# Small unused tiles between the moving tiles of the feed-forward products

## The chip, the core and the metric

The program runs on one core of one Trainium2 chip. The metric is the device time of one execution in microseconds; lower is better. TensorE (PE in the profile) multiplies; VectorE (DVE), ScalarE (ACT) and GpSimd (POOL) work element by element; SyncE (SP) issues most DMAs. Operands lie in SBUF, 128 partitions of some 200 KB each; "an address" below is a tile's byte offset within its partition, the same on all 128.

## The reference, cut to what matters

Two layers, each with a feed-forward, a mixing of tokens (three kinds of attention or recurrence, not touched here), and a second feed-forward. There are 512 tokens, a width of 1024 and an inner width of 2816:

```
def _swiglu(h, wg, wu, wd):
    return (jax.nn.silu(h @ wg) * (h @ wu)) @ wd
...
h = _rmsnorm(x, ffn1_norm[i])
x = x + 0.5 * _swiglu(h, ffn1_w_gate[i], ffn1_w_up[i], ffn1_w_down[i])
h = _rmsnorm(x, mix_norm[i])
x = x + _mixing(h, positions, w_in[i], w_out[i], ...)
h = _rmsnorm(x, ffn2_norm[i])
x = x + 0.5 * _swiglu(h, ffn2_w_gate[i], ffn2_w_up[i], ffn2_w_down[i])
```

All is float32. The four feed-forwards are most of the arithmetic.

## The kernel before

Everything stays transposed: features on the partitions, the 512 tokens along the free axis. To keep float32 precision with a faster product, every operand is split in two float32r tiles, a high part (`xh`, `hh`, `wh`) and the rest (`xl`, `hl`, `wl`), and a product is made of three matmuls (`mm3`, lines 250 to 252): high times high, rest of the data times high weights, and high data times rest of the weights. In each the weights are the stationary operand, a slice of 128 x 128 that one LDWEIGHTS loads, and the data is the moving operand, 128 x 512, that streams past them: 2,048 bytes of each partition, while a slice of weights is 512 bytes.

A feed-forward (`ffn`) has two stages. In the first, for each of 22 blocks of the inner width, the gate and the up product are accumulated (`gu_ps`): 8 slices of the width, three matmuls each, so 24 matmuls for an output and 1,056 for a feed-forward. The moving tiles are the 16 tiles `xh0`, `xl0`, ..., `xh7`, `xl7`. VectorE and ScalarE make the pair `hh`, `hl` of each block out of them. In the second stage, for each of 8 blocks of the width, the down product is accumulated (`d_ps`) over the 22 blocks: 66 matmuls for an output, 528 for a feed-forward; its moving tiles are the 44 tiles `hh0`, `hl0`, ..., `hh21`, `hl21`. `load_split` brings a block of weights (`raw`, three buffers), and ScalarE and VectorE split it (lines 243 and 245) into `wh` and `wl`, two buffers each, of 4,096 bytes; a priority puts these splits ahead of other work, and a scheduler orders the rest.

In the mixing stage the same `xh` and `xl` are the moving operand of `proj_d` (`hf_ps`, `hq_ps`, `fq_ps`, `fk_ps`), 512 columns; in `proj_t` (`hg_ps`, `hi_ps`, `dqk_ps`, `dv_ps`, `fv_ps`) the roles are exchanged: slices of `xh` and `xl` are the stationary operand and a row of `wh` or `wl` of 256 columns moves (260 for `fv_ps`, where a row is 1,040 bytes). The output product (`o_ps`) moves tiles of the mixing stage itself.

The pools lay their tiles one behind another in the order of the code, so addresses follow from sizes. `PAD`, an unused tile at the head of the first pool, shifts all of them together. In the built program they are:

```
        xh0     xl0     xh1    ...  xl7     wh (two)       wl (two)        hh0      hl0      hh1
before  43008   45056   47104  ...  73728   88064, 92160   96256, 100352   124288   126336   128384
after   41696   43776   45856  ...  72896   87232, 91328   95424,  99520   123488   125568   127648
```

Before, the tiles `xh` and `xl` stand whole multiples of 2,048 bytes from the weights, and the tiles `hh` and `hl` multiples of 2,048 plus 1,408. Slices of the weights start every 512 bytes, so what can differ between matmuls is the distance modulo 512: it is 0 for every `xh` and `xl`, and 384 for every `hh` and `hl`. The tiles that `o_ps` moves stand at 128 or 384.

Of the kernel before, what the change touches and what calls it, by code (L numbers as in the profile page):

```python
# [10 lines left out]
F32 = mybir.dt.float32  # L11
# [14 lines left out]
LEVELS = (1, 2, 4, 8, 16, 32, 64)  # L26
AHEAD = 400
CHAIN = 100
PAD = 352


def shape_constants():
# [95 lines left out]
def hybrid_trunk(ctx: ExitStack, tc: tile.TileContext, a, out):  # L128
# [4 lines left out]
    keep = ctx.enter_context(tc.tile_pool(name="keep", bufs=1))  # L133
# [13 lines left out]
    def acc(name):  # L147
        return acc_p.tile([128, 512], F32, tag="acc", name=name)
# [4 lines left out]

    const.tile([128, PAD], F32, name="pad")
    x = [keep.tile([128, T], F32, name=f"x{k}") for k in range(KB)]
# [12 lines left out]
    pos = lines(const, [128, NB], I32, name="pos")  # L168
    xh = [None] * KB
    xl = [None] * KB  # L170

    ones = const.tile([128, 128], F32, name="ones")
    V.memset(ones, 1.0)

    def norm_block(k, g, nrm):

        split_block(k, g)
        square_block(k, nrm)

    def split_block(k, g):  # L180
        xh[k] = keep.tile([128, T], R32, tag=f"xh{k}", name=f"xh{k}")
        S.activation(xh[k], x[k], AF.Copy, scale=g)
        xl[k] = keep.tile([128, T], R32, tag=f"xl{k}", name=f"xl{k}")
        V.scalar_tensor_tensor(out=xl[k], in0=x[k], scalar=g, in1=xh[k].bitcast(F32),  # L184
                               op0=ALU.mult, op1=ALU.subtract)
# [48 lines left out]
    def load_split(src, n, cols):  # L234

        if raws:
            raw = raws.pop(0)
        else:
            raw = wp.tile([128, n, cols], F32, tag="raw", name="raw", bufs=3)
            nc.sync.dma_start(out=raw, in_=src)  # L240
        with tc.high_priority(AHEAD):
            wh = wp.tile([128, n, cols], R32, tag="wh", name="wh")
            S.copy(wh, raw)  # L243
            wl = wp.tile([128, n, cols], R32, tag="wl", name="wl")
            V.tensor_tensor(out=wl, in0=raw, in1=wh.bitcast(F32), op=ALU.subtract)  # L245
        return wh, wl

    def mm3(ps, lh, ll, rh, rl, first, last):

        PE.matmul(ps, lh, rh, start=first, stop=False)  # L250
        PE.matmul(ps, lh, rl, start=False, stop=False)  # L251
        PE.matmul(ps, ll, rh, start=False, stop=last)  # L252
# [8 lines left out]
    for k in range(KB):  # L261
        split_block(k, gvec(("ffn1_norm", 0), k))
# [103 lines left out]
    def ffn(l, wg, wu, wd, after, rb, early=None):  # L366
        with tc.tile_pool(name="ffn", bufs=1, reuse_waits="tile") as fp:
            hh, hl = [], []
            for j in range(FB):
                if j == 4 and early:  # L370
                    early()
                part = []
                for w in (wg, wu):
                    wh, wl = load_split(w[l, j], KB, 128)
                    ps = acc("gu_ps")
                    for k in range(KB):
                        mm3(ps, wh[:, k, :], wl[:, k, :], xh[k], xl[k], k == 0, k == KB - 1)
                    part.append(ps)
                g = fp.tile([128, T], F32, tag="g", name="g", bufs=2)
                V.tensor_tensor(out=g, in0=part[0], in1=rb, op=ALU.mult)  # L380
                S.activation(g, g, AF.Silu)
                u = fp.tile([128, T], F32, tag="u", name="u", bufs=2)
                V.tensor_tensor(out=u, in0=part[1], in1=rb, op=ALU.mult)  # L383
                V.tensor_tensor(out=u, in0=u, in1=g, op=ALU.mult)  # L384
                h1 = fp.tile([128, T], R32, name=f"hh{j}")
                S.copy(h1, u)  # L386
                h2 = fp.tile([128, T], R32, name=f"hl{j}")
                V.tensor_tensor(out=h2, in0=u, in1=h1.bitcast(F32), op=ALU.subtract)  # L388
                hh.append(h1)
                hl.append(h2)  # L390
            for d in range(KB):
                ps = acc("d_ps")
                for j0, j1 in ((0, 8), (8, 15), (15, 22)):
                    wh, wl = load_split(wd[l, d, :, j0:j1, :], j1 - j0, 128)
                    for j in range(j0, j1):
                        mm3(ps, wh[:, j - j0, :], wl[:, j - j0, :], hh[j], hl[j], j == 0, j == FB - 1)
                V.scalar_tensor_tensor(out=x[d], in0=ps, scalar=0.5, in1=x[d], op0=ALU.mult, op1=ALU.add)  # L397
                after(d)
# [361 lines left out]
    for l in range(L):  # L760
        nrm = {}
        ffn(l, a["ffn1_w_gate"], a["ffn1_w_up"], a["ffn1_w_down"],
            lambda d: norm_block(d, gvec(("mix_norm", l), d), nrm), rb, None if l else tables)
        r, rb = norm_finish(nrm)
        nrm = {}
        with ExitStack() as ctx2:
            mixing(l, lambda d: norm_block(d, gvec(("ffn2_norm", l), d), nrm), r, rb)
        r, rb = norm_finish(nrm)
        nrm = {}
        if l + 1 < L:  # L770
            ffn(l, a["ffn2_w_gate"], a["ffn2_w_up"], a["ffn2_w_down"],
                lambda d: norm_block(d, gvec(("ffn1_norm", l + 1), d), nrm), rb)
            r, rb = norm_finish(nrm)
        else:
            def last(d):
                square_block(d, nrm)
                if d == KB - 2:
                    warm = lines(small, [128, 1], tag="warm", name="warm")
                    S.activation(warm, nrm["ss"][:, 0:1], AF.Sqrt)

            ffn(l, a["ffn2_w_gate"], a["ffn2_w_up"], a["ffn2_w_down"], last, rb)
            _, rb = norm_finish(nrm, copy=False)
            for d in range(KB):
                V.scalar_tensor_tensor(out=x[d], in0=x[d], scalar=gvec("final", d), in1=rb,
                                       op0=ALU.mult, op1=ALU.mult)
                (nc.scalar if d % 2 else nc.sync).dma_start(out=out[d * 128:(d + 1) * 128, :], in_=x[d])
# [17 lines left out]
```

## Time and the profile before

| | us |
|---|---|
| median of the two runs | 2114.78 (2114.63 to 2114.94) |
| the profiled execution | 2115.02 |
| its span, first to last instruction | 2113.2 |
| PE busy | 2085.1 (99%) |
| DVE busy | 993.3 (47%) |
| ACT busy | 691.9 (33%) |

The span is the stretch in which the profile sees instructions; the execution has 1.8 us around it. A matmul's duration in the profile is longer than the time it takes from its neighbours, because the next one starts before it has ended: what a matmul costs in a dense stretch is the time from its start to the next one's start, which can be had from the first and the last start of a group and their number.

### The profile page before, as it was taken

To read this page: it belongs to the slowest core of one execution; us is meant where nothing else is said; L and a number is where in the kernel's file an instruction comes from. 1 tells how busy PE (TensorE), PEld (TensorE's weight loads), DVE (VectorE), ACT (ScalarE), POOL (GpSimd) and SP (SyncE) were. 2 spreads that over 40 slices of the span, in tenths; PEclk is the share of its full clock that TensorE was granted. 3 is DMA by queue.
4 is the path that set the end of the run, shared out by engine and by line. 5 is a ranking of instruction groups with operands and counts; after the bars stand their busy time and mean duration, and the time that the engine had idled before them with its cause. 6 is when DMAs were issued, how large, how long until landed. Compare 5 with 4: busy or idle time off the path is not lost.

```text
span 2113.2 us, 25262 instructions
## 1 busy us (share of the span) xinstructions
PE 2085.1 (99%) x10358; PEld 1728.6 (82%) x10358; DVE 993.3 (47%) x1640; ACT 691.9 (33%) x1039; POOL 12.7 (1%) x18
## 2 busy tenths in 40 slices
PE   8999999999999999999999999999999999999997
PEld 6888888889877888888888888889888778888885
DVE  7544433556454544443344443335655454444323
ACT  5323222333443433222233322222344443223221
POOL 0000000000000000000000000000000000000000
PEclk9999999999999999999999999999999999999998
DMA  5333333211122333333333333332111223333332
GB/s 171 100 91 99 95 93 97 90 60 41 31 88 63 94 96 100 100 94 91 95 98 92 100 99 93 93 100 72 60 46 46 65 80 95 100 91 98 93 95 72
DMA packets 55092, 183.71 MB, mean 87 GB/s; under 512 B 7216, under 2 KB 7344, under 8 KB 54976
## 3 DMA queue, kind: packets, MB, share of 16 engines
q1 hardware_dynamic: 54368, 180.98, 28.4%
q8 instruction: 81, 1.33, 0.3%
q10 hardware_dynamic: 576, 1.05, 0.1%
q14 instruction: 35, 0.29, 0.0%
q0 software_dynamic: 32, 0.07, 0.0%
HBM read 179.94 MB, written 2.10 MB: 86 GB/s over the span
## 4 chain that ended last, share of the span: by engine, by line
PE 97%; DVE 1%; ACT 1%; issue 1%; DMA 0%; DVEq 0%; SPq 0%; ACTq 0%
PE gu_ps L251 15%; PE gu_ps L252 15%; PE gu_ps L250 15%; PE d_ps L250 8%; PE d_ps L252 8%; PE d_ps L251 8%; PE lv_ps L510 2%; PE sc_ps L561 2%; PE po L580 2%; PE o_ps L250 1%; PE o_ps L251 1%; PE o_ps L252 1%; PE ho_ps L696 1%; PE pt_ps L573 1%; PE hg_ps L434 1%; PE hg_ps L435 1%
## 5 line engine op out<-in xcount | busy, mean ns | idle before, releaser
L243 ACT CAST wh<-raw 128x1024 fp32r<-128x1024 f32 (+3 forms) x352 | 356.3, 1012 | 1071.7 <-issue 408.4
L245 DVE TENSOR_TENSOR wl<-raw,wh 128x1024 fp32r<-128x1024 f32 (+3 forms) x352 | 413.5, 1175 | 314.0 <-ACT wh L243 311.8
L250 PE MATMUL gu_ps<-xh,wh 128*128 128x512 f32 x1408 | 548.5, 390 | 7.9 <-ACT wh L243 7.9
L252 PE MATMUL gu_ps<-xh,wl 128*128 128x512 f32 x1408 | 550.3, 391 | 0.3 <-DVE wl L245 0.3
L251 PE MATMUL gu_ps<-xl,wh 128*128 128x512 f32 x1408 | 548.0, 390 | 0.0
L250 PEld LDWEIGHTS gu_ps<-xh,wh 128*128 128x128 f32 x1408 | 264.6, 188 | 64.0 <-ACT wh L243 7.9
L252 PEld LDWEIGHTS gu_ps<-xh,wl 128*128 128x128 f32 x1408 | 264.5, 188 | 56.8 <-DVE wl L245 1.5
L251 PEld LDWEIGHTS gu_ps<-xl,wh 128*128 128x128 f32 x1408 | 264.6, 188 | 55.4 <-DVE xl L184 0.2
L252 PE MATMUL d_ps<-hh,wl 128*128 128x512 f32 x704 | 278.1, 395 | 0.0
L250 PE MATMUL d_ps<-hh,wh 128*128 128x512 f32 x704 | 278.1, 395 | 0.0
L251 PE MATMUL d_ps<-hl,wh 128*128 128x512 f32 x704 | 278.1, 395 | 0.0
L383 DVE TENSOR_TENSOR u<-gu_ps,rb 128x512 f32<-128x512 f32 x88 | 60.8, 691 | 269.4 <-PE gu_ps L252 269.4
L252 PEld LDWEIGHTS d_ps<-hh,wl 128*128 128x128 f32 x704 | 132.1, 188 | 32.1
L250 PEld LDWEIGHTS d_ps<-hh,wh 128*128 128x128 f32 x704 | 132.2, 188 | 32.1
L251 PEld LDWEIGHTS d_ps<-hl,wh 128*128 128x128 f32 x704 | 132.2, 188 | 32.0
L380 DVE TENSOR_TENSOR g<-gu_ps,rb 128x512 f32<-128x512 f32 x88 | 60.8, 691 | 177.0 <-PE gu_ps L252 175.1
L386 ACT CAST hh<-u 128x512 fp32r<-128x512 f32 x88 | 54.9, 624 | 64.1 <-DVE u L384 64.1
L397 DVE SCALAR_TENSOR_TENSOR x<-d_ps,x 128x512 f32<-128x512 f32 x32 | 22.1, 691 | 95.4 <-PE d_ps L252 95.4
L384 DVE TENSOR_TENSOR u<-u,g 128x512 f32<-128x512 f32 x88 | 60.9, 692 | 8.3
L388 DVE TENSOR_TENSOR hl<-u,hh 128x512 fp32r<-128x512 f32 x88 | 60.3, 685 | 4.1 <-ACT hh L386 4.1
L510 PE MATMUL lv_ps<-hQ,hk 128*128 128x64 f32 x448 | 54.2, 274 | 2.8 <-DVE hk L521 2.8
L510 PEld LDWEIGHTS lv_ps<-hQ,hk 128*128 128x128 f32 x448 | 52.4, 192 | 5.2 <-PE hi_ps L435 1.3
(242 smaller groups left out, 2360.3 us busy)
## 6 DMA issues: line engine op xcount, KB each, us to landing
raw<-in_ffn_w_gate SPq DMA_DIRECT2D x88, 512.0 KB, 3.5
raw<-in_ffn_w_up SPq DMA_DIRECT2D x88, 512.0 KB, 3.5
raw<-in_ffn_w_down SPq DMA_DIRECT2D x64, 448.0 KB, 3.3
raw<-in_w_in SPq DMA_DIRECT2D x52, 512.0 KB, 3.5
raw<-in_ffn_w_down SPq DMA_DIRECT2D x32, 512.0 KB, 3.5
raw<-in_w_out_dh SPq DMA_DIRECT2D x16, 384.0 KB, 3.0
raw<-in_w_in SPq DMA_DIRECT2D x8, 260.0 KB, 2.7
x<-in_x SPq DMA_DIRECT2D x8, 256.0 KB, 5.7
```

Of the source, the lines that this page charges most:

```text
L243: S.copy(wh, raw)
L245: V.tensor_tensor(out=wl, in0=raw, in1=wh.bitcast(F32), op=ALU.subtract)
L250: PE.matmul(ps, lh, rh, start=first, stop=False)
L251: PE.matmul(ps, lh, rl, start=False, stop=False)
L252: PE.matmul(ps, ll, rh, start=False, stop=last)
L380: V.tensor_tensor(out=g, in0=part[0], in1=rb, op=ALU.mult)
L383: V.tensor_tensor(out=u, in0=part[1], in1=rb, op=ALU.mult)
L384: V.tensor_tensor(out=u, in0=u, in1=g, op=ALU.mult)
L386: S.copy(h1, u)
L388: V.tensor_tensor(out=h2, in0=u, in1=h1.bitcast(F32), op=ALU.subtract)
L510: PE.matmul(ps[:, e:e + 64], K[:, hh, s], Q[:, hh, s].rearrange("p (n two c) -> p n two c", two=2, c=c)[:, :, 1, :], start=True, stop=True)
L561: PE.matmul(ps[:, 0:n], qt(h)[:, b * 128:(b + 1) * 128], kt(h)[:, 0:n], start=True, stop=True)
```

## The change

Tiles of 32 bytes that nothing reads or writes are allocated ahead of every `xh`, `xl`, `hh` and `hl`, and `PAD` goes from 1,408 bytes to 64, which gives room for them. Every such moving tile is now 2,080 bytes behind the one before it. Modulo 512, the distance from the weights is 32 for `xh0`, 64 for `xl0`, 96 for `xh1`, and so on to 0 for `xl7`: each multiple of 32 once. For `hh0` it is 416, for `hl0` 448, and so on through the 44 tiles, each multiple of 32 two or three times. Modulo 64, all tiles stood at 0 before; now `xh` and `hh` stand at 32, and `xl` and `hl` at 0. The tiles of `o_ps` keep their distances from the weights.

```
-PAD = 352
+PAD = 16
...
+    shifted = set()
...
     def split_block(k, g):
+        if k not in shifted:
+            keep.tile([128, 8], F32, name=f"ph{k}")
         xh[k] = keep.tile([128, T], R32, tag=f"xh{k}", name=f"xh{k}")
         S.activation(xh[k], x[k], AF.Copy, scale=g)
+        if k not in shifted:
+            keep.tile([128, 8], F32, name=f"pl{k}")
+            shifted.add(k)
         xl[k] = keep.tile([128, T], R32, tag=f"xl{k}", name=f"xl{k}")
...
+                fp.tile([128, 8], F32, name=f"ph{j}")
                 h1 = fp.tile([128, T], R32, name=f"hh{j}")
                 S.copy(h1, u)
+                fp.tile([128, 8], F32, name=f"pl{j}")
                 h2 = fp.tile([128, T], R32, name=f"hl{j}")
```

No instruction is added to TensorE, ScalarE or SyncE, and on every engine the instructions stand in the same order as before. What is new besides the addresses is one more semaphore that `hl4` waits for on VectorE in the second feed-forward of either layer: its place now overlaps with one that GpSimd has cleared in the mixing stage.

## Rows read from the trace of the kernel before

**Rows 1.** The page: busy time by engine, and the chain that ended last.

```profile
PE 2085.1 (99%) x10358; PEld 1728.6 (82%) x10358; DVE 993.3 (47%) x1640; ACT 691.9 (33%) x1039; POOL 12.7 (1%) x18
...
PE 97%; DVE 1%; ACT 1%; issue 1%; DMA 0%; DVEq 0%; SPq 0%; ACTq 0%
PE gu_ps L251 15%; PE gu_ps L252 15%; PE gu_ps L250 15%; PE d_ps L250 8%; PE d_ps L252 8%; PE d_ps L251 8%; PE lv_ps L510 2%; PE sc_ps L561 2%; PE po L580 2%; PE o_ps L250 1%; PE o_ps L251 1%; PE o_ps L252 1%; PE ho_ps L696 1%; PE pt_ps L573 1%; PE hg_ps L434 1%; PE hg_ps L435 1%
```

**Rows 2.** Busy time of each engine in two stretches of the first feed-forward.

```profile
core 0: us, PE busy (x) PEld busy (x) DVE busy (x) ACT busy (x) POOL busy (x), PEclk, DMA share, GB/s
40.00:240.00 200.00, 200.00 (x884) 165.58 (x884) 99.83 (x160) 63.52 (x81) 0.00 (x0) 1.00 0.32 96
267.00:375.00 108.00, 108.00 (x465) 86.88 (x464) 36.97 (x41) 29.28 (x35) 0.95 (x1) 1.00 0.33 96
```

**Rows 3.** Matmuls into gu_ps, 40 to 240 us: ns min/median/max, first and last start.

```profile
L250 PE MATMUL gu_ps<-xh,wh x295: 389/389/389, 39.8 to 239.7; 128*128 128x512 f32 x148
L251 PE MATMUL gu_ps<-xl,wh x295: 389/389/389, 40.1 to 240.0; 128*128 128x512 f32 x148
L252 PE MATMUL gu_ps<-xh,wl x294: 389/389/389, 40.3 to 239.5; 128*128 128x512 f32 x147
```

**Rows 4.** Matmuls into d_ps, 267 to 375 us.

```profile
L250 PE MATMUL d_ps<-hh,wh x155: 392/392/398, 266.7 to 374.5; 128*128 128x512 f32 x155
L251 PE MATMUL d_ps<-hl,wh x155: 392/398/398, 266.9 to 374.7; 128*128 128x512 f32 x155
L252 PE MATMUL d_ps<-hh,wl x155: 392/392/398, 267.1 to 374.9; 128*128 128x512 f32 x155
```

**Rows 5.** Timeline of PE after a pause, 22.4 to 25.6 us: start, duration.

```profile
22.26 0.36 PE L213 MATMUL ss_ps<-ones,ss 128*128 128x1 f32 x2
22.48 0.48 PE L250 MATMUL gu_ps<-xh,wh 128*128 128x512 f32 x1
22.80 0.40 PE L251 MATMUL gu_ps<-xl,wh 128*128 128x512 f32 x1
23.03 0.40 PE L252 MATMUL gu_ps<-xh,wl 128*128 128x512 f32 x1
...
24.65 0.39 PE L250 MATMUL gu_ps<-xh,wh 128*128 128x512 f32 x1
...
25.55 0.39 PE L251 MATMUL gu_ps<-xl,wh 128*128 128x512 f32 x1
```

**Rows 6.** Matmuls into o_ps, first layer, 615 to 700 us.

```profile
L251 PE MATMUL o_ps<-olA,wh x32: 390/396/481, 622.6 to 683.1; 128*128 128x512 f32 x32
...
L252 PE MATMUL o_ps<-ohd,wl x16: 392/394/690, 621.1 to 680.5; 128*128 128x512 f32 x16
```

**Rows 7.** Matmuls into hf_ps, hi_ps and fv_ps, whole span, by tile.

```profile
L250 PE MATMUL hf_ps<-xh,wh x64: 387/389/578, 375.2 to 1492.1; 128*128 128x512 f32 x64
...
L432 PE MATMUL hi_ps<-wh,xh x128: 277/283/365, 398.9 to 1472.6; 128*128 128x256 f32 x128
...
L432 PE MATMUL fv_ps<-wh,xh x64: 277/282/372, 579.6 to 1636.2; 128*128 128x260 f32 x64
```

**Rows 8.** Matmuls into gu_ps and d_ps, whole span, by tile.

```profile
L250 PE MATMUL gu_ps<-xh,wh x1408: 387/389/796, 7.9 to 1972.8; 128*128 128x512 f32 x176
...
L251 PE MATMUL d_ps<-hl,wh x704: 387/395/399, 252.2 to 2096.2; 128*128 128x512 f32 x176
```

**Rows 9.** Who waited for whom: us in total, times, longest.

```profile
ACT wh L243 <- PE d_ps L251: 274.0, 72, 4.1
DVE u L383 <- PE gu_ps L252: 269.4, 82, 3.4
ACT wh L243 <- PE gu_ps L251: 261.0, 90, 3.4
```

**Rows 10.** Timelines of POOL, 300 to 700 us, and of DVE, 736 to 746 us.

```profile
476.07 0.94 POOL L648 MEMSET fqa<- 2x1024 f32 x1 [11.99 <-DVE hQ L496]
...
737.29 0.69 DVE L388 TENSOR_TENSOR hl<-u,hh 128x512 fp32r<-128x512 f32 x1
```

## The prediction, made before the changed kernel was run

> **What bounds the kernel.** The page comes first: TensorE is busy 99% of the span, and 97% of the chain that ended last is its matmuls, gu_ps and d_ps alone some 68% [rows 1]. The next view asks whether the clock, a DMA or another engine holds it: in both stages of a feed-forward the granted clock is 1.00, so the 2.4 GHz level, PE has no gap, the DMAs are busy about a third of the time, DVE a half and less [rows 2]. The view of waits says the same from the other side: ScalarE, which makes the weights, waits for TensorE to give up a buffer, 261.0 and 274.0 us, and VectorE waits for its results [rows 9]. So each nanosecond on a matmul of a feed-forward is paid in full, and there are 4 x 1,056 = 4,224 into gu_ps and 4 x 528 = 2,112 into d_ps.
>
> What is one worth? The starts tell. In gu_ps, 295 matmuls of line 250 start between 39.8 and 239.7 us, and two others stand between each pair: 199.9 / (294 x 3) = 226.6 ns from start to start; every duration is 389 [rows 3]. In d_ps it is 107.8 / (154 x 3) = 233.3 ns, and the durations are 392 or 398, about half of each [rows 4]. Duration less 162 is the distance to the next start in both (389 gives 227, the mean 395 gives 233), so I read durations in that way below.
>
> The two stages issue the same pair, a load of 128 columns and a matmul of 512, from the same weight buffers, back to back at the same clock. What differs is the place of the moving tile: at distance 0 from the weights (modulo 512) it takes 226.6, at 384 it takes 233.3. That is the best evidence in this trace that the distance has a price, 6.7 ns, which is 16 cycles at 2.4 GHz. The tiles of o_ps, at 128 or 384, show durations of 394 to 396 in the median, thus some 233 ns as well [rows 6].
>
> Distance 0 alone doesn't give the low figure. After a pause, the matmuls into gu_ps that start at 22.80 to 24.65 us take 1.85 / 8 = 231.3 ns each, and only then fall into the even step: 0.90 / 4 = 225, which is 226.6 within the rounding [rows 5]. So there is a settled state at 226.6, reached after some nine matmuls that all stand at the same distance, and a restless one at about 231. All of gu_ps stays settled, as the median of 389 for the whole span shows, with 387 as its smallest [rows 8].
>
> **The change, part by part.** The order of the instructions is the same and TensorE gets none, so nothing is paid for issuing. The new semaphore on hl4 costs nothing: GpSimd's last clearing in the mixing stage starts at 476.07 us and an hl of the second feed-forward is written at 737.29 [rows 10]. Were it late, VectorE's next tensors would queue behind it and then TensorE for its weights, but 260 us cover it. The smaller PAD shifts everything alike; it changes no distance between tiles. Writing the moved tiles is ScalarE's and VectorE's work, which has slack [rows 9].
>
> What remains is the distance. Now two matmuls in a row never have the same one. For gu_ps the trace shows only distance 0; the new ones, each multiple of 32 once, are bounded by the nearest rows: 225 ns (387, the smallest duration seen in either stage) and 236 ns (398, the longer of the two steps of d_ps) [rows 4, 8]. Between them lie 231.3 for matmuls that haven't settled [rows 5] and 233.3 for a settled state at another distance [rows 4]. I expect that a distance which changes with each matmul prevents the settled state at 226.6, and take 232, between these two, as nearest to both. It is a choice; nothing here shows 32, 64 or 96.
>
> - gu_ps: (232 - 226.6) x 4,224 = +22.8 us.
> - d_ps: it loses its 384 for all distances, 0 among them: (232 - 233.3) x 2,112 = -2.7 us.
> - The projections with xh and xl moving, 576 matmuls of 512 columns, have a median of 389 in hf_ps, so about half or more are settled today [rows 7]: 5.4 x 576 x 0.6 = +1.9 us.
> - proj_t, 1,536 matmuls of 256 or 260 columns: the loads are now at other distances. Durations are 283 for hi_ps and, with every second moving row 16 bytes off, 282 for fv_ps, which has 4 columns more [rows 7]. So no price shows there, and I put 0.
> - o_ps keeps its distances: 0.
>
> The sum is +22.0 us on the profiled execution's 2115.02, which is 0.24 over the median of the runs: **2137 us**, 1.0% slower. With the bounds in place of 232, 225 gives -6.8 - 17.5 = -24, so 2091, and 236 gives 39.7 + 5.7 + 3 = +48, so 2163.
>
> **The rivals.**
>
> *No effect: the address isn't what tells gu_ps from d_ps.* Then nothing changes, 2115 us. For it: only two distances are shown, and the stages differ in other things too, such as the number of tiles in turn. Against it: the same instructions, buffers and clock in both. The Trainium skill stands on this side: "SBUF — State Buffer", "Who interferes with whom", gives TensorE two independent read ports, one for the moving operand and one for LDWEIGHTS, and says that it never waits on anyone; "TensorE: Matmul & The Clock Gate", Part 2, says that loading the next weights takes no read bandwidth from the running matmul. By that rule the sum would be 0; rows 3 and 4 don't agree with it as it stands, by 6.7 ns in each matmul. I give this 0.14.
>
> *Faster: another distance takes the load out of the matmul's way.* If a mixture lets most matmuls run like those of 387, gu_ps goes to 225 and d_ps too: 2091 us, as above. For it: such matmuls occur, at distance 0, so the settled 226.6 is no floor [rows 8]. Against it: neither the tiles of o_ps nor those of d_ps have such a median, and over a stretch a short one is made up for by longer ones [rows 4, 5, 6]. For more than 2% one would have to go below the shortest ever seen, to about 222 ns in both. The skill's page on TensorE, Part 1, states 215.7 ns for matmuls of 512 columns without loads between; by an estimate from that page's figure the time would be some 2032 us. I give this rival 0.16, of which 0.04 is over 2%.
>
> *Slower by over 2%: every matmul takes the longer step.* The d_ps stage alternates 392 and 398, which is what two matmuls in turn can do when their distance is the same [rows 4]. When the distance moves on by 32 bytes with each matmul, the short step may never come: (236 - 226.6) x 4,224 + (236 - 233.3) x 2,112 + 3 = +48, 2163 us. With the 399 that d_ps reaches once [rows 8], 237 ns, it is +55, 2170. It decides from gu_ps at about 236 ns on, since 2% is 42 us. That xh and hh now start half-way in a piece of 64 bytes could be its cause. For it: half of d_ps is in that state today. Against it: in no group is 398 the median of all three lines, and at 16 bytes off fv_ps shows nothing. I give it 0.18.
>
> **How the numbers follow.** The forecast, gu_ps between 229 and 235 ns, has 0.52. The range is 2100 to 2165: it takes in the forecast (2122 to 2152), no effect, the milder part of the faster case and the near half of the slower one; outside it I leave some 0.06 below and 0.12 above. A measurement of this kernel can tell about 2% from no change, 2072.5 or 2157: faster by more 0.04, slower by more 0.18, within it 0.78.
>
> **What would show it.** The durations of gu_ps and d_ps by tile: gu_ps should leave the constant 389 for a mixture of 387 to 398 with a mean near 394, d_ps should leave its two values for a similar mixture with about the same mean, and the starts of each stage should then stand 232 ns apart. o_ps and proj_t should keep their medians, PE its 99%, and the waits of ScalarE for TensorE should grow with gu_ps. If gu_ps stays at 389 the address of the moving tile isn't the cause; if it goes to 387 or to a value never seen here, the bounds were too narrow, above all because distances below 128 have no row. I am wrong, too, if absolute places count: PAD moved the weights from multiples of 2,048 to multiples of 64.

## The result, and the profile after

| | us |
|---|---|
| before, median | 2114.78 (2114.63 to 2114.94) |
| changed kernel, median of 2 | 2138.39 (2137.82 to 2138.95) |
| ratio | 1.0111, 95% interval 1.0092 to 1.0129 |
| the profiled execution, and its span | 2138.95, 2137.1 |

The changed kernel is 1.1% slower, 23.6 us; 2137 was forecast. The 95% interval of the ratio leaves out 1, so the difference is clear of the noise, though it is under 2%.

The page of the changed kernel, busy time by engine and the chain that ended last, answers to [rows 1]:

```profile
PE 2109.0 (99%) x10358; PEld 1731.1 (81%) x10358; DVE 993.7 (46%) x1640; ACT 691.5 (32%) x1039; POOL 12.7 (1%) x18
...
PE 98%; DVE 1%; ACT 0%; issue 0%; DMA 0%; SPq 0%; DVEq 0%; ACTq 0%
```

The count of matmuls is the same, and only PE's busy time has grown, by 23.9 us, which is the growth of the span (2113.2 to 2137.1). Busy time by stretch answers to [rows 2]:

```profile
40.00:240.00 200.00, 200.00 (x863) 161.70 (x862) 98.20 (x159) 62.17 (x79) 0.00 (x0) 1.00 0.31 94
258.00:373.00 115.00, 115.00 (x497) 92.98 (x496) 41.15 (x46) 31.65 (x38) 0.00 (x0) 1.00 0.32 93
```

The granted clock is still 1.00 in both stages and PE has no gap, but the same 200 us of gu_ps hold 863 matmuls where there were 884. TensorE doesn't wait longer; each of its matmuls takes longer. The durations by tile say how (ns min/median/max, first and last start; the lines 250 to 252 are now 256 to 258), for gu_ps from 40 to 240 us and d_ps from 258 to 373, against [rows 3] and [rows 4]:

```profile
L256 PE MATMUL gu_ps<-xh,wh x288: 392/396/399, 39.6 to 239.7; 128*128 128x512 f32 x144
L257 PE MATMUL gu_ps<-xl,wh x288: 387/393/400, 39.9 to 240.0; 128*128 128x512 f32 x144
L258 PE MATMUL gu_ps<-xh,wl x287: 389/395/399, 40.1 to 239.5; 128*128 128x512 f32 x144
...
L256 PE MATMUL d_ps<-hh,wh x166: 392/397/399, 257.9 to 372.9; 128*128 128x512 f32 x166
L257 PE MATMUL d_ps<-hl,wh x165: 387/393/400, 258.1 to 372.5; 128*128 128x512 f32 x165
L258 PE MATMUL d_ps<-hh,wl x165: 389/395/399, 258.3 to 372.7; 128*128 128x512 f32 x165
```

The constant 389 of gu_ps is gone: durations run from 387 to 400. From start to start it is 200.1 / (287 x 3) = 232.4 ns, where it was 226.6. In d_ps, 392 or 398 before, the same mixture stands, and 115.0 / (165 x 3) = 232.3 ns, where it was 233.3. The two stages are now alike, as they should be if the place of the moving tile made them different.

The mixing stage (hf_ps, hi_ps and fv_ps over the whole span, and o_ps of the first layer, against [rows 6] and [rows 7]):

```profile
L256 PE MATMUL hf_ps<-xh,wh x64: 389/396/582, 380.6 to 1508.9; 128*128 128x512 f32 x64
...
L440 PE MATMUL hi_ps<-wh,xh x128: 274/281/367, 404.7 to 1489.2; 128*128 128x256 f32 x128
...
L440 PE MATMUL fv_ps<-wh,xh x64: 278/283/368, 585.0 to 1654.3; 128*128 128x260 f32 x64
...
L257 PE MATMUL o_ps<-olA,wh x32: 388/396/479, 628.4 to 688.8; 128*128 128x512 f32 x32
```

hf_ps has left its median of 389 like gu_ps; hi_ps is 2 ns shorter, fv_ps 1 longer, and o_ps, whose distances are kept, is where it was.

The view of waits, against [rows 9], and the timelines of POOL and DVE, against [rows 10]:

```profile
DVE u L389 <- PE gu_ps L258: 281.1, 82, 3.5
ACT wh L249 <- PE gu_ps L257: 273.8, 91, 3.7
ACT wh L249 <- PE d_ps L257: 272.7, 72, 4.0
```

```profile
481.85 0.94 POOL L656 MEMSET fqa<- 2x1024 f32 x1 [12.08 <-DVE hQ L504]
...
743.97 0.69 DVE L396 TENSOR_TENSOR hl<-u,hh 128x512 fp32r<-128x512 f32 x1
```

In these rows VectorE and ScalarE wait 12 and 13 us longer for gu_ps, and ScalarE 1 us less for d_ps: TensorE is still the one that is waited for. GpSimd's last clearing still ends some 260 us before the hl shown, the fourth of the second feed-forward; hl4, the one that could wait for it, is the next.

### The profile page after: what moved, and what is told of

Same layout as the page of the kernel before. It is cut to its first block, busy times and chain, and to the rows that moved or that the text cites. A ratio compares the mean times of both kernels' runs of the same rounds, so it can differ in the third digit from the quotient of the medians.

```text
span 2137.1 us, 25264 instructions
## 1 busy us (share of the span) xinstructions
PE 2109.0 (99%) x10358; PEld 1731.1 (81%) x10358; DVE 993.7 (46%) x1640; ACT 691.5 (32%) x1039; POOL 12.7 (1%) x18
## 4 chain that ended last, share of the span: by engine, by line
PE 98%; DVE 1%; ACT 0%; issue 0%; DMA 0%; SPq 0%; DVEq 0%; ACTq 0%
PE gu_ps L256 15%; PE gu_ps L258 15%; PE gu_ps L257 15%; PE d_ps L256 8%; PE d_ps L258 8%; PE d_ps L257 8%; PE lv_ps L518 2%; PE sc_ps L569 2%; PE po L588 2%; PE o_ps L256 1%; PE o_ps L257 1%; PE o_ps L258 1%; PE ho_ps L704 1%; PE pt_ps L581 1%; PE hg_ps L442 1%; PE hg_ps L443 1%
## 5 line engine op out<-in xcount | busy, mean ns | idle before, releaser
L256 PE MATMUL gu_ps<-xh,wh 128*128 128x512 f32 x1408 | 557.7, 396 | 8.1 <-ACT wh L249 8.1
L258 PE MATMUL gu_ps<-xh,wl 128*128 128x512 f32 x1408 | 558.3, 397 | 0.0
L257 PE MATMUL gu_ps<-xl,wh 128*128 128x512 f32 x1408 | 554.5, 394 | 0.0
```

## The experiments

All times are medians; "before" beside them is the kernel before on the same chip. My theory: what a matmul costs depends on the distance of its moving tile from the weights, modulo 256 or 512 bytes. The rivals: absolute places; the change from tile to tile, whatever the distances; or something else in d_ps than its address.

**1. Absolute places.** PAD alone, no tiles between. In the first run everything moves by 1,344 bytes, a multiple of 64; in the second by 1,376, so that everything starts 32 bytes past a multiple of 64.

```
-PAD = 352
+PAD = 16        (e1_pad64)
+PAD = 8         (e1_pad32)
```

> The kernel before with PAD at 64 bytes and no tiles between: every address moves down by 1,344 bytes, no distance changes. My theory (the distance of the moving tile from the weights tells): 226.6 ns from start to start in gu_ps and 233.3 in d_ps as before, 2115 us. Rival (absolute places tell, the weights are no longer at multiples of 2,048): gu_ps goes to 231 to 233, 2135 to 2140 us.

> The kernel before with PAD at 32 bytes: every tile moves by the same amount, data and weights now both start at 32 modulo 64, no distance changes. My theory (distances alone tell): 2115 us and 226.6 and 233.3 ns. Rival (a start that isn't a multiple of 64 costs by itself, and explains why xh and hh at 32 modulo 64 were restless): gu_ps goes to 231 ns or more, over 2130 us.

Measured 2115.16 us (ratio 1.0003, interval 0.9993 to 1.0013; before 2114.73) and 2115.45 (1.0003, 0.9993 to 1.0013; before 2114.64). By tile, a line each for gu_ps (40 to 240 us) and d_ps (267 to 375 us), first of e1_pad64, then of e1_pad32:

```profile
L250 PE MATMUL gu_ps<-xh,wh x295: 389/389/389, 39.8 to 239.7; 128*128 128x512 f32 x148
...
L250 PE MATMUL d_ps<-hh,wh x154: 392/395/398, 267.3 to 374.4; 128*128 128x512 f32 x154
...
L250 PE MATMUL gu_ps<-xh,wh x295: 388/389/390, 39.7 to 239.6; 128*128 128x512 f32 x148
...
L251 PE MATMUL d_ps<-hl,wh x155: 392/393/399, 266.7 to 374.5; 128*128 128x512 f32 x155
```

That is 226.6 and 233.3 ns, as before, in both runs. In e1_pad32, with all operands at 32 modulo 64, gu_ps has durations of 388 to 390 and still 295 starts in 199.9 us. So the smaller PAD has no part in the result, and neither has a start half-way in 64 bytes. What is left is the distance between the operands.

**2. The two halves of the change.** Tiles before xh and xl alone, and before hh and hl alone.

```
e2_xh_only, against the changed kernel:      e2_hh_only, against the kernel before:
-  fp.tile([128, 8], F32, name=f"ph{j}")     +  fp.tile([128, 8], F32, name=f"ph{j}")
-  fp.tile([128, 8], F32, name=f"pl{j}")     +  fp.tile([128, 8], F32, name=f"pl{j}")
                                             -PAD = 352
                                             +PAD = 16
```

> The change without the tiles before hh and hl: xh and xl stand in steps of 32, hh and hl all at 384. My theory: gu_ps as in the changed kernel, 232.4 ns, d_ps as before, 233.3: 2115 + 23.4 + 2 = 2140 us. Rival (the stages act on one another, the restless state is carried over from one to the next): d_ps leaves its two values 392 and 398.

> The change without the tiles before xh and xl: hh and hl stand in steps of 32, xh and xl all at 0. My theory: gu_ps 226.6 ns, d_ps 232.4 instead of 233.3: 2115 - 1.9 = 2113 us. Rival (the stages act on one another): gu_ps is restless in the stages that follow a d_ps, and the time lies over 2120.

Measured 2138.49 us (ratio 1.0111, 1.0096 to 1.0127) and 2113.83 (0.9995, 0.9986 to 1.0004; before 2114.73). The whole loss comes with xh and xl. In e2_hh_only gu_ps keeps its 389, so nothing is carried into it from d_ps, and d_ps takes 106.0 / (152 x 3) = 232.5 ns; its time is 0.9 us lower, which the interval can't tell from nothing. In e2_xh_only, however, d_ps isn't as before, although all hh and hl stand at 384 as they did (both from 267 to 373 us, e2_hh_only first):

```profile
L250 PE MATMUL d_ps<-hh,wh x153: 392/396/398, 266.7 to 372.7; 128*128 128x512 f32 x153
...
L258 PE MATMUL d_ps<-hh,wl x153: 390/393/404, 266.7 to 372.6; 128*128 128x512 f32 x153
L256 PE MATMUL d_ps<-hh,wh x153: 390/393/404, 266.9 to 372.9; 128*128 128x512 f32 x153
L257 PE MATMUL d_ps<-hl,wh x152: 390/393/404, 267.1 to 372.4; 128*128 128x512 f32 x152
```

Instead of 392 and 398 there are durations from 390 to 404, and again 106.0 / (152 x 3) = 232.5 ns. So this rival was right in part: at one and the same distance d_ps can run in two sequences, and which one goes with what ran before (experiment 4 has it again). It is worth 1 ns in a matmul, some 2 us in all, which is why 2138.5 came where 2140 was expected.

**3. Is it the address that makes d_ps slower?** One unused tile, no steps.

```
                 V.tensor_tensor(out=u, in0=u, in1=g, op=ALU.mult)
+                if j == 0:
+                    fp.tile([128, 160], F32, name="align")
                 h1 = fp.tile([128, T], R32, name=f"hh{j}")
```

> The kernel before with one unused tile of 640 bytes ahead of hh0, so that all hh and hl stand at multiples of 2,048 from the weights, like xh and xl. My theory: d_ps settles at 226.6 ns with a constant duration of 389: 2,112 x 6.7 = 14.1 us less, 2100.7 us. Rival (d_ps is slower for another reason than its address, 44 tiles instead of 16 or the length of its accumulation): 233.3 as before, 2115 us.

> The kernel with the unused tile of 640 bytes ahead of hh0 once more, beside the one above on the same chip: 2100.7 us by my theory, with 226.67 ns in both stages. Rival (the gain depends on the chip): anything between 2100 and 2115.

Measured 2100.65 us (0.9935, 0.9919 to 0.9952; before 2114.73), and again 2100.66 (0.9933, 0.9920 to 0.9947; before 2114.64). d_ps from 267 to 373 us:

```profile
L250 PE MATMUL d_ps<-hh,wh x153: 389/389/389, 266.8 to 370.1; 128*128 128x512 f32 x153
L251 PE MATMUL d_ps<-hl,wh x153: 389/389/389, 267.0 to 370.4; 128*128 128x512 f32 x153
L252 PE MATMUL d_ps<-hh,wl x153: 389/389/389, 267.2 to 370.6; 128*128 128x512 f32 x153
```

With 44 tiles and 66 matmuls for an output, d_ps settles at the constant 389 and at 103.3 / (152 x 3) = 226.5 ns. It was the address. This kernel beats both.

**4. The other stage at the distance of d_ps.**

```
+    keep.tile([128, 32], F32, name="off")      (behind xl7, ahead of the weights)
-PAD = 352
+PAD = 320
```

> The kernel before with 128 unused bytes between xl7 and the weights (and PAD smaller by as much): all xh and xl stand at 384 modulo 512, as hh and hl do. My theory: gu_ps takes on the two values of d_ps, 392 and 398, and 233.3 ns: 4,224 x 6.7 = 28 us more, with the projections some 31: 2146 us. Rival (only a change of distance from tile to tile costs, the value doesn't): gu_ps settles at 226.6, 2115 us.

Measured 2137.73 us (1.0105, 1.0076 to 1.0134; before 2115.58). gu_ps from 40 to 240 us, and d_ps from 267 to 373:

```profile
L252 PE MATMUL gu_ps<-xh,wl x288: 390/393/404, 39.8 to 239.9; 128*128 128x512 f32 x144
...
L251 PE MATMUL d_ps<-hl,wh x153: 390/393/404, 266.8 to 372.8; 128*128 128x512 f32 x153
```

The distance 384 slows gu_ps as well, with all its tiles at one distance, and the rival by which only a change of distance costs is refuted. But it takes 200.1 / (287 x 3) = 232.4 ns with the durations of 390 to 404, not the 392 and 398 expected, and d_ps falls to 232.5 with the same durations, though its tiles and the weights stand where they stood before. So 5.8 x 4,224 - 0.8 x 2,112 = +22.8 us, and 22.2 were measured: hence 2138 and not 2146. A constant 384 costs gu_ps as much as the steps of 32.

**5. A price list by distance.** All hh and hl of a feed-forward at one distance, another in each of the four; then cut out of one tile, at distances under 32 and at 48.

```
+    places = iter(((32, 0), (40, 0), (48, 0), (56, 0)))      (floats ahead of hh0; e6 likewise)
...
+        head, step = next(places)
...
+                if j == 0 and head:
+                    fp.tile([128, head], F32, name="head")
                 h1 = fp.tile([128, T], R32, name=f"hh{j}")
```

> The kernel before with all hh and hl of a feed-forward at one distance, another one in each of the four: 0, 32, 64, 96 modulo 512. Start to start in d_ps, theory (a price by distance that is 0 at 0 and 16 cycles at 128, growing evenly): 226.6, 228.3, 230, 231.7 ns. Rival (any distance but 0 costs the same): 226.6, then 233.3 three times. Second rival (every constant distance settles, and only 384 is bad): 226.6 four times.

> As before, with the distances 160, 192, 224, 256 in the four feed-forwards. Theory (period of 256, price growing evenly with the distance): 235, 236.7, 238.3, 226.6 ns. Rival (any distance but 0 modulo 256 costs the same): 233.3 three times, then 226.6. Second rival (period of 512): the last one isn't 226.6 but 233 or more.

> The kernel before with all hh and hl cut out of one tile, at distances 4, 8, 16 and 48 modulo 512 in the four feed-forwards. So far 0 and 256 give 226.67, 64 gives 228.9, and 32, 96, 192, 224 give 233.33. Theory now (any distance inside the 256 but 0 has a price, 64 an exception): 233 in all four. Rival (the price belongs to pieces of 16 or 32 bytes, a start inside the first piece is free): 226.67 for 4 and 8, perhaps 16, and 228 to 234 for 48.

These three are single runs. Matmuls into d_ps by tile, one line for each of the four feed-forwards. e5_hh_0_32_64_96:

```profile
L252 PE MATMUL d_ps<-hh,wl x176: 388/389/390, 252.8 to 371.8; 128*128 128x512 f32 x176
...
L250 PE MATMUL d_ps<-hh,wh x171: 393/396/398, 930.8 to 1049.8; 128*128 128x512 f32 x171
...
L250 PE MATMUL d_ps<-hh,wh x169: 393/394/395, 1296.7 to 1412.0; 128*128 128x512 f32 x169
...
L251 PE MATMUL d_ps<-hl,wh x167: 393/394/395, 1974.6 to 2090.8; 128*128 128x512 f32 x167
```

e6_hh_160_192_224_256:

```profile
L250 PE MATMUL d_ps<-hh,wh x173: 392/397/400, 252.8 to 373.6; 128*128 128x512 f32 x173
...
L252 PE MATMUL d_ps<-hh,wl x174: 394/394/394, 930.8 to 1051.9; 128*128 128x512 f32 x174
...
L252 PE MATMUL d_ps<-hh,wl x174: 395/396/396, 1296.7 to 1417.8; 128*128 128x512 f32 x174
...
L250 PE MATMUL d_ps<-hh,wh x173: 389/389/389, 1974.8 to 2091.8; 128*128 128x512 f32 x173
```

e9_hh_4_8_16_48 (the one tile is called flat):

```profile
L250 PE MATMUL d_ps<-flat,wh x170: 397/402/403, 252.8 to 373.5; 128*128 128x512 f32 x170
...
L250 PE MATMUL d_ps<-flat,wh x172: 389/396/398, 932.2 to 1051.3; 128*128 128x512 f32 x172
...
L250 PE MATMUL d_ps<-flat,wh x175: 390/392/398, 1296.8 to 1417.7; 128*128 128x512 f32 x175
...
L251 PE MATMUL d_ps<-flat,wh x168: 395/396/396, 1974.6 to 2091.5; 128*128 128x512 f32 x168
```

From the first and the last start of each line, by (last - first) / (3 x (count - 1)):

| distance | 0 | 4 | 8 | 16 | 32 | 48 | 64 | 96 | 160 | 192 | 224 | 256 |
|---|---|---|---|---|---|---|---|---|---|---|---|---|
| ns | 226.7 | 238.1 | 232.2 | 231.6 | 233.3 | 233.3 | 228.8 | 233.3 | 234.1 | 233.3 | 233.3 | 226.7 |

The 128 that is missing can be read from 384, if the period is 256: 233.3 or 232.5. 256 is as good as 0, so the rival with 512 falls. A period of 256 bytes fits the changed kernel too: from 40 to 240 us, the mean time from a matmul's start to the next one's is 233.2, 234.4, 231.7 and 232.6 ns for those on xh0 to xh3, and the same four numbers for those on xh4 to xh7, which stand 256 bytes further modulo 512. That the price grows evenly falls too, since 32 already has all of it; so does the idea that a start inside the first 16 or 32 bytes is free, since 4 is the dearest of all. What I said at the last, 233 wherever it isn't 0 or 64, held for 48 alone of these four. The times agree: for e5 the mean of its four is 230.5 ns, 2.8 under 233.3, so -5.9 us on the 2115.58 of the kernel before on that chip, and 2109.6 was measured (e6 2111.44 on the same chip; e9 2115.7, where the kernel before took 2114.64).

**6. Steps of other sizes.**

```
+    places = iter(((32, 64), (32, 32), (32, 16), (40, 64)))
...
+                if j and step:
+                    fp.tile([128, step], F32, name=f"ph{j}")
...
+                if step:
+                    fp.tile([128, step], F32, name=f"pl{j}")
```

> The kernel before with hh and hl in steps of another size in each feed-forward: 256 bytes from 0, 128 from 0, 64 from 0, and 256 from 32. Theory (what counts is the distance modulo 256, and a change of it bars the settled state): 226.6 ns with a constant duration in the first, some 232 in the second and the third, and in the fourth what a constant 32 gives. Rival (each step from tile to tile bars it, whatever its size): 232 in all four.

Measured 2108.36 us, one run (before 2115.58). d_ps by tile, one line for each feed-forward:

```profile
L252 PE MATMUL d_ps<-hh,wl x176: 388/389/390, 252.7 to 371.7; 128*128 128x512 f32 x176
...
L250 PE MATMUL d_ps<-hh,wh x171: 388/389/390, 930.6 to 1047.4; 128*128 128x512 f32 x171
...
L252 PE MATMUL d_ps<-hh,wl x166: 392/394/398, 1296.8 to 1411.2; 128*128 128x512 f32 x166
...
L251 PE MATMUL d_ps<-hl,wh x165: 393/395/397, 1974.8 to 2089.6; 128*128 128x512 f32 x165
```

Steps of 256 from 0 leave 226.7 ns; steps of 256 from 32 cost 233.3, what a constant 32 costs; steps of 128 give 229.0 and of 64 give 231.1. The mean of the four is 230.0, 3.3 under 233.3, so -7.0 us, as the time shows. So a step as such bars nothing: it counts through the distances modulo 256 that it makes. In the steps of 128, for one, all hh stand at 0 and all hl at 128 modulo 256; two matmuls in three move an hh, and (2 x 226.7 + 233.3) / 3 is 228.9. The expected 232 for the steps of 128 and 64 was too high.

**7. The mixing stage as well.** hh and hl at 0 as in 3, and:

```
         mp = ctx2.enter_context(tc.tile_pool(name="mix", bufs=1, reuse_waits="tile"))
+        mp.tile([128, 32], F32, name="align")
-PAD = 352
+PAD = 320
```

> The kernel with hh and hl at 0, and 128 unused bytes at the head of the mixing stage's pool (PAD smaller by as much), so that the tiles of o_ps stand at 0 or 256 too. My theory: the 384 matmuls into o_ps fall from some 233 to 226.6 ns where nine or more follow each other; most don't: between 0 and 2.4 us less than with hh and hl alone, 2098 to 2101 us. Rival (some other pair of the mixing stage loses what o_ps gains): over 2102 us.

Measured 2100.04 us (0.9930, 0.9916 to 0.9943) beside 2100.66 for hh and hl alone on the same chip. o_ps of the first layer:

```profile
L251 PE MATMUL o_ps<-olA,wh x32: 388/391/483, 619.9 to 679.9; 128*128 128x512 f32 x32
```

The median falls from 396 to 391, in the direction that was expected; the 0.6 us in the time can't be told from nothing, since the intervals overlap. The rival, over 2102 us, falls.

## Why the prediction was right

- *The bound.* A nanosecond on a matmul is paid in full: shown by the result, where the span and PE's busy time grew by the same 23.9 us, and by experiment 3, where 6.7 ns on 2,112 matmuls, 14.1 us, came back as 14.1.
- *The distance is the cause.* The prediction argued it from one pair of stages; it is shown by experiments 1, 3 and 4, which keep all distances, bring d_ps to the distance of gu_ps, and the reverse. The rival without effect falls with them. The page "SBUF — State Buffer" of the Trainium skill, which stood on its side, has TensorE never wait on anyone; these runs measured 6.7 ns between distances 384 and 0 with the same instructions, and the measurement decides.
- *gu_ps at 232.* It is 232.4: 5.8 x 4,224 = +24.5 by the rows, +22.8 forecast. Added up from start to start over the whole trace, gu_ps grows by 23.4 us: that all of it was settled before was a little too strong, since its mean was 227.9 with the matmuls after pauses. The value was chosen between 231.3 and 233.3, and that it was hit so closely is in part luck, because the reason given, that a changing distance prevents the settled state, was only half right. By experiment 6 steps of 256 are harmless, and by experiment 4 a constant distance of 384 is as dear. Of the distances that were run, those that aren't a multiple of 256 all bar 226.7, changing or not, and 232 is nearly the mean of the price list: two matmuls in three move an xh, at 32, 96, 160 or 224 modulo 256, one an xl, at 0, 64, 128 or 192, and by that weight the list, with 384 read as 128, gives 232.4 to 232.5. The other half stands: in the changed kernel the matmuls on xl3 and xl7, at 256 and 0, take 231.4 ns to the next start on average (40 to 240 us), not 226.7, so in this mixture a good distance loses its low price.
- *d_ps, -2.7.* It fell from 233.3 to 232.3, -2.1 (added up over the trace, -1.9).
- *The projections with xh and xl, +1.9.* Added up from start to start, the four grow by 1.8; hf_ps has left its 389. *proj_t and o_ps, 0*: hi_ps 2 ns shorter, fv_ps 1 longer, o_ps at its place, and added up, under 0.1 us for either.
- *The hidden wait.* hl4 costs nothing: what it could wait for is done over 260 us earlier, as forecast.
- *The faster rival* didn't come: no distance went below 226.7 over a stage. *The slower one*, every matmul at the longer step, didn't either: 398 to 400 are the ends of a mixture. Its supposed cause, a start half-way in 64 bytes, is refuted by e1_pad32. Yet a distance with such a price exists: 4 bytes, 238.1.

What stays open is why. That the pattern belongs to two reads of one memory that meet, the load's and the matmul's, is only argued. One rival, that the matmul meets the writes of VectorE and ScalarE (to the next weights, for one), has a row of the kernel before against it:

```profile
304.77 1.09 DVE L245 TENSOR_TENSOR wl<-raw,wh 128x896 fp32r<-128x896 f32 x1 [3.29 <-ACT wh L243]
...
306.11 0.40 PE L251 MATMUL d_ps<-hl,wh 128*128 128x512 f32 x1
...
308.44 0.40 PE L252 MATMUL d_ps<-hh,wl 128*128 128x512 f32 x1
308.64 1.05 ACT L243 CAST wh<-raw 128x1024 fp32r<-128x1024 f32 x1 [3.91 <-PE d_ps L251]
```

From the end of the first row's work, at 305.86 us, to the start of the last row's neither engine works, and the ten steps of d_ps there still take 2.33 us, 233 ns each. The DMAs run on, so they aren't excluded. Own weights and next weights stand at the same distance modulo 256 in all these runs, so which of them counts can't be said, and nor can why 64 is cheap and 160 dear.

## What to carry to other kernels

Where TensorE is busy without a gap and each matmul has its own load (here 512 columns after a load of 128, in float32r), look at the start-to-start time of each stage, not at the busy share: two stages with the same instructions and different steps are a sign. Then look at the addresses of the operands, not only at their sizes: here a multiple of 256 bytes between the moving tile and the weights was best in both stages, and one unused tile of 640 bytes gave 0.65% where 60 tiles of 32 bytes cost 1.1%. Spreading the operands over all distances came out near the mean price; putting them at one good distance got the best.

## What the runs showed that I had not expected

- A period of 256 bytes, as far as it was tried, with a price that isn't even inside it: 226.7 at 0, 238.1 at 4, 231.6 at 16, 228.8 at 64, 233.3 at 32, 48, 96, 192 and 224, 234.1 at 160.
- Two sequences at one distance: at 384 d_ps ran at 233.3 ns (392 and 398) behind a settled gu_ps and at 232.5 ns (390 to 404) behind a restless one, over its whole length; in experiment 4 the weights, hh and hl have the same addresses as in the kernel before.
- A settled stage shows 389 throughout in some kernels and 388 to 390 in others with the same mean: in e1_pad32, but in e5_hh_0_32_64_96 too, at distance 0 with PAD as before. The addresses don't decide it: e3_hh_at_0 and e10_hh_at_0_again are one program on two chips, and d_ps shows 389 throughout in the first and 388 to 390 in the second. What it comes from stays open.
